# Right sides of the second token phase made ahead and kept in DRAM, and bias tables written by a job of their own

## The chip, the cores and the metric

The kernel runs on one core of a Trainium2 chip. TensorE (PE), VectorE (DVE), ScalarE (ACT), GpSimd (POOL) and SyncE (SP) each execute their instructions in the order of their own queue. The metric is device microseconds from one execution of the whole program.

## The reference

One step of a decoder layer for 1024 prompt tokens and 64 sample tokens of width 1024, 1088 columns in all. What matters here is the feed-forward block, which runs once before and once after the attention part:

```python
def _rmsnorm(x, g):
    y = xf * lax.rsqrt(jnp.mean(xf * xf, axis=-1, keepdims=True) + EPS)
    return (y * g.astype(jnp.float32)).astype(x.dtype)

def _swiglu(x, w_up, w_down):
    gate, up = jnp.split(x @ w_up, 2, axis=-1)
    return (jax.nn.silu(gate) * up) @ w_down
...
x = x + 0.5 * _swiglu(_rmsnorm(x, w["norm_ffn1"]), w["ffn1_w_up"], w["ffn1_w_down"])
... # attention with relative position bias, pooling, gates
x = x + 0.5 * _swiglu(_rmsnorm(x, w["norm_ffn2"]), w["ffn2_w_up"], w["ffn2_w_down"])
```

The attention adds a bias that is looked up in `rel_bias_table` by distance. Hidden width is 2816, everything is float32.

## The kernel before, in words

**Numbers.** A float32 operand is split into a rounded part and a rest (hi and lo, `split`, L217 on ACT and L218 on DVE or POOL), and a product is made of three matmuls, hi·hi, hi·lo and lo·hi (`mm3`, L271 to L273).

**Feed-forward block.** The residual `xt` lies transposed in SBUF, 8 blocks of 128 rows by 1088 columns. The columns are worked in two phases, `PHASES = ((0, 256), (512, 288))`: phase 0 takes columns 0 to 511 as two halves of 256, phase 1 columns 512 to 1087 as two halves of 288. Each phase runs over 22 units, 44 in the block; a unit takes 256 columns of the up weights, alternately of the gate and of the up half, and `jj` counts pairs of units, 0 to 21. A unit is a 2 × 2 block product in Strassen's manner, with 7 products instead of 8. Product q (0 to 6) multiplies a left side, a sum or difference of weight blocks, by a right side, a sum or difference of blocks of the normalised tokens; each is 12 matmuls (3 for each of k = 0 to 3), 84 a unit.

- *Left sides* are made by `prepare`, `LEAD = 5` products ahead of their use: at q = 0 POOL adds and subtracts (L435, L436), at q = 2 again (L439, L440), and each left side is rounded by ACT into `sh` and its rest made by DVE (`sl<-ur`, `sl<-s`, L218).
- *Right sides* are the same for all 22 units of a phase. `right_sides` makes them once at the start of a phase and keeps them in the SBUF buffers `h_hi` and `h_lo`, 7 q by 4 k by 256 or 288 columns. Per k it forms four halves (token block times gain times row scale, L382 on DVE, the row scale read from PSUM, where `over_rows`, L351, put it), four differences (L389, one on DVE and three on POOL) and seven splits (L394 on ACT, L395 on DVE, one of seven on POOL). So with phase 1 the whole of `h_hi`/`h_lo` is written anew, after the last product of phase 0 has read it. The sums of squares behind the phase-1 row scale (`sumsq`, L312 to L318) are made earlier, by two jobs started at `jj == 1`.
- *Results.* Products are combined on DVE (L516, L520, L522, L528, L529, L533) to the hidden values, which are split into `hh` and `hl` (`hl` on POOL). A pair of units later `down` multiplies them by the down weights into `psb`, in 512-column (phase 1: 288-column) matmuls, and L479 on DVE adds the sum to `xt`. After the last pair of phase 0 all its downs follow at once, and then `right_sides` of phase 1. SP issues the weight loads; `wh`/`wl` are down weights split by ACT and POOL.

`psa` and `psb` are PSUM tiles with four banks each, `tmp` a ring of eight SBUF tiles.

**Bias tables.** At the start `biases` makes four small matmuls (L570) of a one-hot table and `rel_bias_table`, copies them (`fr`, L572) and stores them to DRAM (`f_scr`, L573). From there POOL's queue issues 44 small DMAs into `b_scr` (L627, L629, L632, L635) and three larger ones into `f_rep` (L639), which the attention part reads long after the first block.

**What sets the order.** Python code emits instructions in program order, in which an `Interleaver` runs jobs beside the main code: its clock is advanced by the main code (0.36 us for a k of a product and so on), and a job that yields n is continued n us later on that clock. A scheduler then reorders the instructions of each engine by its own estimate of the time, so that the place in the code doesn't settle the place in a queue.

Of the kernel before, what the change touches and what calls it, by code (L numbers as in the profile page):

```python
# [11 lines left out]
F32 = mybir.dt.float32  # L12
F32R = mybir.dt.float32r
# [7 lines left out]
P = 128  # L21
# [98 lines left out]
def body(ctx, tc, x_prompt, x_sample, c128, c512, c2048, state_pool, rel_bias_table,  # L120
# [21 lines left out]
    def psa():  # L142
        return ps.tile([P, 512], F32, tag="a", name="psa")
# [39 lines left out]
    a_scr = dr.tile([P, 2, T], F32, name="a_scr")  # L183
    b_scr = dr.tile([3, NS, 4, 192], F32, name="b_scr")
    f_scr = dr.tile([4, 4, BL], F32, name="f_scr")
    f_rep = dr.tile([4, 4, P, BL], F32, name="f_rep")

    last_load = [None]
# [184 lines left out]
    def right_sides(xt, gi, p, rs):  # L373
# [23 lines left out]
        for k in range(4):  # L397
# [10 lines left out]
            parts(6, k, b22)  # L408
            parts(5, k, t4, G)

    def ffn(xt, gi, w_up, w_down, hook):


# [35 lines left out]
        def product(i, p):  # L449
            while made[0] <= i + LEAD:  # L450
                prepare(made[0])
                made[0] += 1
            lh, ll = left.pop(i)
            bank = psa()[:, :PHASES[p][1]]
            mm3(bank, [(lh[:, k, :], ll[:, k, :], *operand(p, i % 7, k)) for k in range(4)],
                0.36)
            il.advance(0.36)
            return bank
# [33 lines left out]

        load_unit(0)
        load_unit(1)
        prev = None
        for jj in range(22):
            p, j = divmod(jj, 11)
            t0, m = PHASES[p]
            if j == 0:
                if p:  # L500
                    right_sides(xt, gi, p, [over_rows(diagonal(st, m)) for st in sts])
                prev = None
            if jj == 1:
                sts = [stat() for _ in range(2)]
                for h in range(2):
                    il.spawn(sumsq(xt, PHASES[1][0] + h * PHASES[1][1], PHASES[1][1], sts[h]), 8 * h)
            hid = [fp.tile([P, 2, 576], F32R, tag=x, name=x, bufs=2) for x in ("hh", "hl")]
            sil = {}
            for kind in range(2):
# [30 lines left out]
                result(0, 1, product(7 * n + 6, p), b, False)  # L540
            prev = hid
            if j == 10 and p == 0:
                down_some(jj, prev, range(KD))
            elif j == 10:
                hook(jj, -1, 0)
                for i, (c0, n) in enumerate(chunks(1)):
                    for d in range(KD):
                        down(jj, prev, d, c0, n)
                        hook(jj, i, d)
# [30 lines left out]
    for t in range(ntile):  # L580
        rows = P if t < 8 else NS
        xn = ip.tile([P, D], F32, tag="xn", name="xn", bufs=7)
        load(xn[:rows], xp[t * P:(t + 1) * P, :] if t < 8 else xs)
        xns.append(xn)
    first = []
    for tiles in ((0, 1), (2, 3), (4, 5, 6, 7, 8)):
        for t in tiles:
# [27 lines left out]
        first.append(over_rows(dg))  # L615
        if tiles[0] == 2:
            right_sides(xt, 0, 0, first)
    biases()
    ictx.close()
    bctx.close()  # L620

    def fbias(g, off, ap):
        return bass.AP(tensor=f_scr.tensor, offset=f_scr.offset + g * 4 * BL + off, ap=ap)


    for g in range(3):
        G.dma_start(out=b_scr[g][:, :, P:], in_=neg.unsqueeze(1).to_broadcast([NS, 4, NS]))  # L627
        if g == 2:
            G.dma_start(out=b_scr[g][:, :, :P], in_=fbias(g, 127, [[0, NS], [BL, 4], [1, P]]))  # L629
        else:  # L630
            for q in range(Q):
                G.dma_start(out=b_scr[g][q::Q, :, :P],  # L632
                            in_=fbias(g, 127 - q // DIL[g], [[0, B], [BL, 4], [1, P]]))
        for b in range(B):
            G.dma_start(out=b_scr[g][b * Q:(b + 1) * Q, :, P + b * Q:P + (b + 1) * Q],  # L635
                        in_=fbias(g, 384, [[Q, Q], [BL, 4], [1, Q]]))

    for g in (0, 1, 3):
        G.dma_start(out=f_rep[g], in_=fbias(g, 0, [[BL, 4], [0, P], [1, BL]]))  # L639

    def spill(c):
        c0, n = CH[c]
# [794 lines left out]
```

## Time and profile before

| | |
|---|---|
| Median of 3 runs | 2520.71 us (2518.93 to 2524.88) |
| The profiled execution, own time | 2517.62 us |
| Its span, first to last instruction | 2515.9 us |
| Mean granted clock of TensorE | 0.953 |
| Busy: PE, DVE, POOL, ACT | 94%, 72%, 45%, 39% |
| First block, phase change | 438 to 494 us |
| Second block, phase change | 2068.4 to 2120.2 us |
| Up-weight loads | 176 of 512 KB, 3.9 us each to landing |
| Down-weight loads | 88 of 512 KB, 5.7 us each to landing |

Times are microseconds. The profiled execution stands beside the runs' median; durations are read from it. Busy shares are means over the whole span, and single stretches differ from them. The clock is given as a share of full speed (1 is 2.4 GHz, 0.5 is 1.2 GHz).

### The profile page before, as it was taken

What the parts mean: (1) busy time and instruction counts of PE and PEld (TensorE: products, weight loads), DVE (VectorE), ACT (ScalarE), POOL (GpSimd) and SP (SyncE); (2) the same over time, 40 slices, a digit from 0 to 9 for tenths busy, and PEclk for the clock granted to TensorE, in tenths of its full rate; (3) what the DMA queues carried; (4) which work ended last, traced back from release to release, by engine and by line L of the source; (5) the groups of instructions that cost most, each with busy time, mean ns of one, the idle gap of its engine ahead of it and who ended that gap; (6) DMA issues with size and microseconds to landing.
All of it is one profiled execution on the core that took longest, in us unless ns stands there. A gap on an engine that the chain in (4) does not pass through costs nothing. (4 is left out here: it accounts for less than half of the span.)

```text
span 2515.9 us, 42145 instructions
## 1 busy us (share of the span) xinstructions
PE 2363.3 (94%) x15894; PEld 2235.3 (89%) x15894; DVE 1817.6 (72%) x3246; ACT 975.9 (39%) x2130; POOL 1136.1 (45%) x1060
## 2 busy tenths in 40 slices
PE   4499999799999989999999999997999998999999
PEld 2489998699999989999999889996899987999998
DVE  5498888788888863366677424629988888788886
ACT  4244444343443433344333222214444443444442
POOL 6656666556555431201011110105666665566554
PEclk7799999799999989999899999997999997999999
DMA  6223343333324122457565773622244432333251
GB/s 189 78 80 109 109 134 134 124 101 118 118 101 134 50 68 83 152 163 233 181 193 177 244 233 118 217 76 75 88 140 140 152 138 68 126 127 127 92 201 38
DMA packets 208314, 328.72 MB, mean 131 GB/s; under 512 B 16272, under 2 KB 171600, under 8 KB 207328
## 3 DMA queue, kind: packets, MB, share of 16 engines
q1 hardware_dynamic: 194096, 293.48, 35.6%
q0 software_dynamic: 14016, 32.56, 3.7%
q8 instruction: 125, 2.05, 0.3%
q14 instruction: 77, 0.63, 0.1%
HBM read 297.10 MB, written 76.32 MB: 148 GB/s over the span
## 5 line engine op out<-in xcount | busy, mean ns | idle before, releaser
L271 PE MATMUL psa<-h_hi,sh 128*128 128x256 f32 (+1 forms) x2464 | 724.9, 295 | 62.1 <-ACT sh L217 51.0
L272 PE MATMUL psa<-h_lo,sh 128*128 128x256 f32 (+1 forms) x2464 | 727.9, 295 | 18.7 <-DVE h_lo L395 18.3
L273 PE MATMUL psa<-h_hi,sl 128*128 128x256 f32 (+1 forms) x2464 | 723.1, 294 | 0.0
L218 DVE TENSOR_TENSOR sl<-ur,sh 128x512 fp32r<-128x512 f32 x528 | 589.5, 1123 | 109.9 <-ACT sh L217 99.9
L271 PEld LDWEIGHTS psa<-h_hi,sh 128*128 128x128 f32 x2464 | 474.2, 193 | 77.4 <-ACT sh L217 52.8
L272 PEld LDWEIGHTS psa<-h_lo,sh 128*128 128x128 f32 x2464 | 474.7, 193 | 33.6 <-DVE h_lo L395 29.3
L273 PEld LDWEIGHTS psa<-h_hi,sl 128*128 128x128 f32 x2464 | 475.6, 193 | 0.5 <-DVE sl L218 0.5
L217 ACT ACTIVATE sh<-ur 128x512 fp32r<-128x512 f32 x528 | 330.3, 627 | 370.3 <-POOL ur L439 187.2
L272 PE MATMUL psa<-h_lo,wh 128*128 128x360 f32 (+1 forms) x1104 | 374.7, 339 | 5.5 <-DVE h_lo L364 5.5
L271 PE MATMUL psa<-h_hi,wh 128*128 128x360 f32 (+1 forms) x1104 | 376.6, 342 | 3.4 <-ACT h_hi L363 3.4
L273 PE MATMUL psa<-h_hi,wl 128*128 128x360 f32 (+1 forms) x1104 | 370.9, 336 | 0.0
L272 PE MATMUL psb<-hl,wh 128*128 128x288 f32 (+1 forms) x1056 | 349.0, 331 | 6.2 <-POOL hl L218 6.2
L271 PE MATMUL psb<-hh,wh 128*128 128x288 f32 (+1 forms) x1056 | 338.0, 336 | 13.3 <-ACT hh L217 11.5
L273 PE MATMUL psb<-hh,wl 128*128 128x288 f32 (+1 forms) x1056 | 348.5, 331 | 0.0
L218 POOL TENSOR_TENSOR hl<-tmp,hh 128x288 fp32r<-128x288 f32 (+1 forms) x176 | 171.7, 984 | 378.4 <-ACT hh L217 378.4
L479 DVE SCALAR_TENSOR_TENSOR xt<-psb,xt 128x288 f32<-128x288 f32 (+1 forms) x528 | 260.8, 526 | 76.2 <-PE psb L273 75.3
L218 POOL TENSOR_TENSOR wl<-wr,wh 128x512 fp32r<-128x512 f32 x176 | 259.0, 1492 | 93.5 <-ACT wh L217 49.2
L217 ACT ACTIVATE wh<-wr 128x512 fp32r<-128x512 f32 (+1 forms) x284 | 157.9, 615 | 177.9 <-PE psa L272 112.9
L272 PEld LDWEIGHTS psa<-h_lo,wh 128*128 128x128 f32 x1104 | 214.2, 194 | 10.3 <-DVE h_lo L364 5.8
L271 PEld LDWEIGHTS psa<-h_hi,wh 128*128 128x128 f32 x1104 | 213.6, 194 | 10.6 <-issue 5.0
L271 PEld LDWEIGHTS psb<-hh,wh 128*128 128x128 f32 x1056 | 194.9, 190 | 29.4 <-ACT hh L217 12.4
L272 PEld LDWEIGHTS psb<-hl,wh 128*128 128x128 f32 x1056 | 200.7, 190 | 22.4 <-POOL hl L218 8.6
(262 smaller groups left out, 3416.9 us busy)
## 6 DMA issues: line engine op xcount, KB each, us to landing
ur<-in_ffn_w_up_dram SPq DMA_DIRECT2D x176, 512.0 KB, 3.9
wr<-in_ffn_w_down_dram SPq DMA_DIRECT2D x88, 512.0 KB, 5.7
out_dram<-in_cache_kv_w_dram SPq DMA_DIRECT2D x32, 1020.0 KB, 7.6
qb<-q_scr SPq DMA_DIRECT2D x96, 256.0 KB, 4.4
wr<-in_w_in_dram SPq DMA_DIRECT2D x38, 512.0 KB, 4.7
kt<-in_cache_kv_w_dram SPq DMA_DIRECT2D x64, 256.0 KB, 4.3
vt<-in_cache_kv_w_dram SPq DMA_DIRECT2D x26, 512.0 KB, 7.9
t<-t_scr SPq DMA_DIRECT2D x16, 544.0 KB, 5.0
```

The lines of the kernel that those rows point to most:

```text
L217: S.activation(hi, src, AF.Copy)
L218: eng.tensor_tensor(out=lo, in0=src, in1=hi.bitcast(F32), op=ALU.subtract)
L271: PE.matmul(out, lh, rh, start=i == 0, stop=False)
L272: PE.matmul(out, lh, rl, start=False, stop=False)
L273: PE.matmul(out, ll, rh, start=False, stop=i == n - 1)
L479: V.scalar_tensor_tensor(out=xd, in0=o, scalar=0.5, in1=xd, op0=ALU.mult, op1=ALU.add)
```

## The change

**Right sides.** A new job `staged`, started at `jj == 1`, replaces the two `sumsq` jobs and the call of `right_sides` for phase 1. It makes the sums of squares, copies the row scale of each half from PSUM to an SBUF tile `rr`, and then forms per k, in three steps that yield 12 each, eight halves (L427: `b12` is formed three times, `b22` twice, `b11` twice, `b21` once), five differences (L433) and seven splits, all differences and rests on DVE. Each split goes to one of three rotating 288-column slots that lie in `h_hi`/`h_lo` behind the phase-0 right sides (28 × 256 = 7168 columns; the slots take 3 × 288 of the rest), and two DMAs on POOL's queue store it to a new DRAM tensor `r_scr` (144 KB each, 56 in a block). `recalled(q)` loads right side q into its place in `h_hi`/`h_lo`, two DMAs of 576 KB on POOL's queue: q = 0 to 4 before the products q = 2 to 6 of the last unit of phase 0, q = 5 and 6 after it. Both feed-forward blocks do so.

**Tables.** `biases` is called before the transposes of the tokens, and the 47 table DMAs are issued by a job `tables`, which starts 30 us into the interleaver's clock and yields 2 after each.

```diff
+    r_scr = dr.tile([2, 7, P, 4, PHASES[1][1]], F32R, name="r_scr")
...
+    def staged(xt, gi, rr):
+
+        t0, m = PHASES[1]
+        hi_, lo_ = [x.rearrange("p k t -> p (k t)") for x in (h_hi, h_lo)]
+        free = 28 * PHASES[0][1]
+        sts = [stat(), stat()]
+        for s in range(2):
+            yield from sumsq(xt, t0 + s * m, m, sts[s])
+            yield 8
+            V.tensor_copy(rr[:, s * m:(s + 1) * m], over_rows(diagonal(sts[s], m)))
+            yield 8
+        slot = [0]
+
+        def half(k, s):
+            h = tmp()[:, :m]
+            V.scalar_tensor_tensor(out=h, in0=xt[:, k, t0 + s * m:t0 + s * m + m],
+                                   scalar=gains[:, gi, k:k + 1], in1=rr[:, s * m:(s + 1) * m],
+                                   op0=ALU.mult, op1=ALU.mult)
+            return h
+
+        def less(a, b):
+            V.tensor_tensor(out=a, in0=a, in1=b, op=ALU.subtract)
+
+        def keep(q, k, h):
+            o = free + slot[0] % 3 * m
+            slot[0] += 1
+            hi, lo = hi_[:, o:o + m], lo_[:, o:o + m]
+            split(hi, lo, h)
+            G.dma_start(out=r_scr[0, q][:, k, :], in_=hi)
+            G.dma_start(out=r_scr[1, q][:, k, :], in_=lo)
+
+        for k in range(4):
+            b11, b12 = half(k, 0), half(k, 1)
+            keep(0, k, b11)
+            less(b12, b11)
+            keep(3, k, b12)
+            yield 12
+            b22, b12 = half(k + 4, 1), half(k, 1)
+            keep(6, k, b22)
+            less(b22, b12)
+            keep(4, k, b22)
+            yield 12
+            b22, b12 = half(k + 4, 1), half(k, 1)
+            less(b12, half(k, 0))
+            less(b22, b12)
+            keep(2, k, b22)
+            b21 = half(k + 4, 0)
+            keep(1, k, b21)
+            less(b21, b22)
+            keep(5, k, b21)
+            yield 12
+
+    def recalled(q):
+        m = PHASES[1][1]
+        for i, x in enumerate((h_hi, h_lo)):
+            G.dma_start(out=x.rearrange("p k t -> p (k t)")[:, 4 * q * m:4 * (q + 1) * m],
+                        in_=r_scr[i, q].rearrange("p k m -> p (k m)"))
...
             lh, ll = left.pop(i)
+            if 7 * 21 < i < 7 * 22:
+                recalled(i % 7 - 2) if i % 7 > 1 else None
...
             if j == 0:
-                if p:
-                    right_sides(xt, gi, p, [over_rows(diagonal(st, m)) for st in sts])
                 prev = None
             if jj == 1:
-                sts = [stat() for _ in range(2)]
-                for h in range(2):
-                    il.spawn(sumsq(xt, PHASES[1][0] + h * PHASES[1][1], PHASES[1][1], sts[h]), 8 * h)
+                job = il.spawn(staged(xt, gi, fp.tile([P, 576], F32, name="rr")))
+            if jj == 10:
+                il.finish(job)
...
             if j == 10 and p == 0:
+                recalled(5)
+                recalled(6)
                 down_some(jj, prev, range(KD))
...
+    biases()
     first = []
...
-    biases()
...
-    for g in (0, 1, 3):
-        G.dma_start(out=f_rep[g], in_=fbias(g, 0, [[BL, 4], [0, P], [1, BL]]))
+    def tables():
...
+        for g in (0, 1, 3):
+            G.dma_start(out=f_rep[g], in_=fbias(g, 0, [[BL, 4], [0, P], [1, BL]]))
+            yield 2
+
+    il.spawn(tables(), 30)
```

**Where the instructions come to stand.** The line numbers of the changed kernel are one higher up to the new functions and some 60 higher behind them: L218/L219 are its `split`, L272 to L274 its `mm3`, L390 and L396 the differences and rests of `right_sides`, L494, L495, L498, L499 the additions of the left sides, L540 the sum into `xt`, L575 to L592 the combinations, L690 to L705 the table writes.

At the start, on POOL, from the end of the table writes on; before (`s_497` and `ur` are weights and weight sums of the first unit):

```order
44 L635 DMA b_scr<-f_scr 32x1x8 x5
45 L629 DMA b_scr<-f_scr 256x1x128
46 L635 DMA b_scr<-f_scr 32x1x8 x7
47 L395 TENSOR_TENSOR h_lo<-tmp,h_hi 128x256
48 L635 DMA b_scr<-f_scr 32x1x8
49 L639 DMA f_rep<-f_scr 512x1x448 x2
50 L435 TENSOR_TENSOR s_497<-ur 128x512
51 L436 TENSOR_TENSOR ur<-ur 128x4x128
52 L439 TENSOR_TENSOR ur<-s_497,ur 128x4x128
53 L440 TENSOR_TENSOR ur<-ur 128x4x128
```

and in the changed kernel, where `s_451` is the sum of the first unit:

```order
33 L700 DMA b_scr<-f_scr 32x1x8 x5
34 L495 TENSOR_TENSOR ur<-ur 128x4x128
35 L700 DMA b_scr<-f_scr 32x1x8 x3
36 L396 TENSOR_TENSOR h_lo<-tmp,h_hi 128x256
37 L390 TENSOR_TENSOR tmp<-tmp 128x256
38 L705 DMA f_rep<-f_scr 512x1x448 x2
39 L390 TENSOR_TENSOR tmp<-tmp 128x256
40 L705 DMA f_rep<-f_scr 512x1x448
41 L498 TENSOR_TENSOR ur<-s_451,ur 128x4x128
42 L390 TENSOR_TENSOR tmp<-tmp 128x256 x2
43 L396 TENSOR_TENSOR h_lo<-tmp,h_hi 128x256
44 L499 TENSOR_TENSOR ur<-ur 128x4x128
```

The f_rep issues are still ahead of the second pair of additions of the first unit (L439 before, L498 now), and the differences and rests of the right sides, which stood among the table writes, now partly follow them.

In phase 0, on DVE, one unit from its last rest of a weight sum on; before:

```order
220 L218 TENSOR_TENSOR sl<-s_1723,sh 128x512
221 L479 SCALAR_TENSOR_TENSOR xt<-psb,xt 128x512 x4
222 L516 TENSOR_TENSOR si<-tmp,psa 128x256
223 L218 TENSOR_TENSOR sl<-ur,sh 128x512
224 L516 TENSOR_TENSOR si<-tmp,psa 128x256
225 L218 TENSOR_TENSOR sl<-ur,sh 128x512 x2
226 L520 TENSOR_TENSOR tmp<-tmp,psa 128x256
227 L522 TENSOR_TENSOR tmp<-tmp,si 128x256
228 L218 TENSOR_TENSOR sl<-ur,sh 128x512
229 L528 TENSOR_TENSOR tmp<-tmp,psa 128x256
230 L218 TENSOR_TENSOR sl<-ur,sh 128x512
```

and the same place of the changed kernel, a unit in which the job works:

```order
242 L219 TENSOR_TENSOR sl<-s_1745,sh 128x512
243 L219 TENSOR_TENSOR sl<-ur,sh 128x512
244 L540 SCALAR_TENSOR_TENSOR xt<-psb,xt 128x512
245 L219 TENSOR_TENSOR sl<-ur,sh 128x512
246 L540 SCALAR_TENSOR_TENSOR xt<-psb,xt 128x512 x3
247 L579 TENSOR_TENSOR tmp<-tmp,psa 128x256
248 L427 SCALAR_TENSOR_TENSOR tmp<-xt,gains,rr 128x288 x2
249 L581 TENSOR_TENSOR tmp<-tmp,si 128x256
250 L587 TENSOR_TENSOR tmp<-tmp,psa 128x256
251 L433 TENSOR_TENSOR tmp<-tmp 128x288
252 L219 TENSOR_TENSOR h_lo<-tmp,h_hi 128x288
253 L588 TENSOR_TENSOR tmp<-tmp,psa 128x256
```

Halves (L427), a difference (L433) and rests into the slots (`h_lo<-tmp,h_hi`) now stand between the combinations and the rests of the left sides. On POOL the two stores of each split stand between additions in the same way.

At the phase change of the first block, on PE, the last downs of phase 0 and what follows; before:

```order
2361 L271 MATMUL psb<-hh,wh 128x512
2362 L272 MATMUL psb<-hl,wh 128x512
2363 L273 MATMUL psb<-hh,wl 128x512
2364 L351 MATMUL psb<-tmp,ones 128x288 x2
2365 L271 MATMUL psa<-h_hi,sh 128x288 x2
2366 L272 MATMUL psa<-h_lo,sh 128x288
2367 L273 MATMUL psa<-h_hi,sl 128x288
2368 L272 MATMUL psa<-h_lo,sh 128x288
2369 L273 MATMUL psa<-h_hi,sl 128x288
```

and in the changed kernel:

```order
2341 L272 MATMUL psa<-h_hi,sh 128x288
2342 L273 MATMUL psa<-h_lo,sh 128x288
2343 L274 MATMUL psa<-h_hi,sl 128x288
2344 L272 MATMUL psb<-hh,wh 128x512 x4
2345 L272 MATMUL psa<-h_hi,sh 128x288
2346 L273 MATMUL psa<-h_lo,sh 128x288
2347 L274 MATMUL psa<-h_hi,sl 128x288
2348 L272 MATMUL psa<-h_hi,sh 128x288
2349 L273 MATMUL psa<-h_lo,sh 128x288
```

Product 0 of phase 1 (288 columns) now precedes downs of phase 0 (`psb`, 512 columns), which before came first, all 48 of them; five of the new phase's products stand ahead of the last of them. On POOL, at the same place, the loads into `h_hi` and `h_lo` in the changed kernel:

```order
238 L494 TENSOR_TENSOR s_4782<-ur 128x512
239 L495 TENSOR_TENSOR ur<-ur 128x4x128
240 L467 DMA h_lo<-r_scr 128x1152
241 L467 DMA h_hi<-r_scr 128x1152
242 L467 DMA h_lo<-r_scr 128x1152
243 L467 DMA h_hi<-r_scr 128x1152
244 L219 TENSOR_TENSOR hl<-tmp,hh 128x256
245 L498 TENSOR_TENSOR ur<-s_4782,ur 128x4x128
246 L467 DMA h_lo<-r_scr 128x1152
247 L467 DMA h_hi<-r_scr 128x1152
248 L499 TENSOR_TENSOR ur<-ur 128x4x128
249 L467 DMA h_lo<-r_scr 128x1152
```

They stand between the additions of the next units' left sides (L494 to L499) and the rests `hl` of the hidden values; the last four come some nine rows later, behind four `wl`. Before, differences and rests of the right sides stood there.

## Rows read from the trace of the kernel before

**Rows 1.** Page: busy time of each engine; PE's busy tenths in 40 slices.
```profile
PE 2363.3 (94%) x15894; PEld 2235.3 (89%) x15894; DVE 1817.6 (72%) x3246; ACT 975.9 (39%) x2130; POOL 1136.1 (45%) x1060
...
PE   4499999799999989999999999997999998999999
```

**Rows 2.** Timeline of PE near 96 us: start, us, instruction, [idle before <-releaser].
```profile
95.80 0.58 PE L271 MATMUL psa<-h_hi,sh 128*128 128x256 f32 x1 [35.39 <-ACT sh L217]
```

**Rows 3.** Timeline of POOL, 18 to 95 us.
```profile
18.89 2.69 POOL L218 TENSOR_TENSOR wl<-wr,wh 128x512 fp32r<-128x512 f32 x2 [8.07 <-ACT wh L217]
...
36.56 3.35 POOL L632 DMA_DIRECT2D b_scr<-f_scr  x6 [0.72 <-DMA f_scr<-fr]
...
50.11 0.76 POOL L389 TENSOR_TENSOR tmp<-tmp 128x256 f32<-128x256 f32 x1
...
64.58 0.55 POOL L632 DMA_DIRECT2D b_scr<-f_scr  x1 [9.96 <-DMA f_rep<-f_scr]
...
90.03 1.09 POOL L639 DMA_DIRECT2D f_rep<-f_scr  x1 [11.59 <-issue]
91.13 1.28 POOL L435 TENSOR_TENSOR s<-ur 128x512 f32<-128x512 f32 x1
```

**Rows 4.** Windows: us, PE PEld DVE ACT POOL busy (x), clock, DMA share, GB/s.
```profile
438.00:494.00 56.00, 38.87 (x142) 29.69 (x142) 44.60 (x68) 19.74 (x45) 31.09 (x31) 0.73 0.34 120
200.00:420.00 220.00, 220.00 (x1523) 204.38 (x1522) 186.50 (x284) 99.72 (x197) 148.03 (x112) 1.00 0.37 123
520.00:840.00 320.00, 320.00 (x2392) 318.13 (x2391) 269.38 (x435) 130.64 (x252) 184.49 (x144) 1.00 0.33 112
```

**Rows 5.** Windows of PE's psa instructions (two rows), then of its psb instructions (one).
```profile
438.00:494.00 56.00, 23.86 (x90) 0.73 0.34 120
2068.40:2120.20 51.80, 21.79 (x68) 0.67 0.29 102
...
438.00:494.00 56.00, 15.01 (x52) 0.73 0.34 120
```

**Rows 6.** Timeline of PE around the first phase change.
```profile
442.63 1.66 PE L271 MATMUL psb<-hh,wh 128*128 128x512 f32 x4 [4.58 <-ACT hh L217]
445.91 0.79 PE L272 MATMUL psb<-hl,wh 128*128 128x512 f32 x1 [1.62 <-POOL hl L218]
...
450.42 0.40 PE L273 MATMUL psb<-hh,wl 128*128 128x512 f32 x1
...
457.90 0.40 PE L273 MATMUL psb<-hh,wl 128*128 128x512 f32 x1
458.13 1.13 PE L351 MATMUL psb<-tmp,ones 128*128 128x288 f32 x4
```

**Rows 7.** Timeline of DVE at the same place.
```profile
458.94 1.78 DVE L382 SCALAR_TENSOR_TENSOR tmp<-xt,gains,psb 128x288 f32<-128x288 f32 x4
...
468.38 0.45 DVE L395 TENSOR_TENSOR h_lo<-tmp,h_hi 128x288 fp32r<-128x288 f32 x1
```

**Rows 8.** DVE's groups, 438 to 494: count | busy us, mean ns | idle before.
```profile
L395 DVE TENSOR_TENSOR h_lo<-tmp,h_hi 128x288 fp32r<-128x288 f32 x24 | 19.7, 859 | 0.0
```

**Rows 9.** Groups of DVE's instructions, 200 to 420.
```profile
L218 DVE TENSOR_TENSOR sl<-ur,sh 128x512 fp32r<-128x512 f32 x85 | 93.9, 1111 | 11.8 <-ACT sh L217 11.0
...
L522 DVE TENSOR_TENSOR tmp<-tmp,si 128x256 f32<-128x256 f32 x28 | 16.7, 596 | 0.7
L520 DVE TENSOR_TENSOR tmp<-tmp,psa 128x256 f32<-128x256 f32 x28 | 11.7, 418 | 10.4 <-PE psa L273 10.4
```

**Rows 10.** Line L218, 200 to 420: duration ns min/median/max.
```profile
L218 DVE TENSOR_TENSOR sl<-ur,sh x85: 678/900/1810, 199.3 to 417.2; 128x512 fp32r<-128x512 f32 x85
...
L218 POOL TENSOR_TENSOR hl<-tmp,hh x28: 736/963/1201, 209.0 to 413.6; 128x256 fp32r<-128x256 f32 x28
L218 POOL TENSOR_TENSOR wl<-wr,wh x28: 1291/1610/1744, 218.1 to 410.7; 128x512 fp32r<-128x512 f32 x28
```

**Rows 11.** Windows, the first 20 us (columns as in rows 4).
```profile
0.00:20.00 20.00, 9.18 (x45) 7.98 (x46) 9.27 (x45) 10.08 (x18) 8.81 (x17) 1.00 0.93 297
```

More of the change, by code (lines that the diff above doesn't have):

```diff
@@ L494, in ffn @@
         load_unit(1)
-        prev = None
+        prev = job = None
         for jj in range(22):
@@ L623, in fbias @@
         return bass.AP(tensor=f_scr.tensor, offset=f_scr.offset + g * 4 * BL + off, ap=ap)
[L626 to L636, printed above, removed]
-    for g in (0, 1, 3):
-        G.dma_start(out=f_rep[g], in_=fbias(g, 0, [[BL, 4], [0, P], [1, BL]]))
+    def tables():
+        for g in range(3):
+            G.dma_start(out=b_scr[g][:, :, P:], in_=neg.unsqueeze(1).to_broadcast([NS, 4, NS]))
+            if g == 2:
+                G.dma_start(out=b_scr[g][:, :, :P], in_=fbias(g, 127, [[0, NS], [BL, 4], [1, P]]))
+                yield 2
+            else:
+                for q in range(Q):
+                    G.dma_start(out=b_scr[g][q::Q, :, :P],
+                                in_=fbias(g, 127 - q // DIL[g], [[0, B], [BL, 4], [1, P]]))
+                    yield 2
+            for b in range(B):
+                G.dma_start(out=b_scr[g][b * Q:(b + 1) * Q, :, P + b * Q:P + (b + 1) * Q],
+                            in_=fbias(g, 384, [[Q, Q], [BL, 4], [1, Q]]))
+                yield 2
+        for g in (0, 1, 3):
+            G.dma_start(out=f_rep[g], in_=fbias(g, 0, [[BL, 4], [0, P], [1, BL]]))
+            yield 2
+    il.spawn(tables(), 30)
     def spill(c):
```

## The prediction

> **What bounds the kernel now.** I read the page first: TensorE (PE) is busy 94% of the span, VectorE (DVE) 72%, GpSimd (POOL) 45% [rows 1]. A PE that is nearly always busy is shortened only where it stands still or runs at the lower clock, and the slices say where: the first two, one in each feed-forward block at its change of token phase, and the two ends of the middle part [rows 1]. The change touches three such places.
>
> *The start.* PE's timeline shows a wait of 35.39 us up to 95.80, for a left side that ScalarE (ACT) rounds [rows 2]. The timeline of POOL shows why. Left sides of products 2 onward need the additions L435 to L439, and these stand on POOL behind the table writes: b_scr issues of 0.55 us each, the first f_rep issue, then 9.96 us of waiting for its transfer, more issues, a second wait of 11.59 us ahead of the last f_rep issue, and only at 91.13 the first L435 [rows 3].
>
> *The two phase changes.* In the window 438–494 PE works 38.87 us of 56.00 at a mean granted clock of 0.73; in its twin, 2068.4–2120.2, the clock is 0.67 [rows 4, 5]. The reader should first ask what this work costs at full speed. From 520 to 840 PE is busy without a gap, with 2392 matmuls of 288 columns: 320/2392 = 0.134 us each [rows 4]. The 33 down matmuls of 512 columns from 450.42 to 457.90 stand 7.48/32 = 0.234 us apart [rows 6]. The first window holds 90 product matmuls and 52 on psb, four of them L351 and 48 downs, so 90 × 0.134 + 48 × 0.234 = 23.3 us; the second has 68 and, by the code, again 48 downs, so 9.1 + 11.2 = 20.3 [rows 5, 6]. Lost are **32.7 and 31.5 us**. The timeline puts it in three pieces: 4.58 and 1.62 us for the hidden values; downs at the lower clock until about 450; and after the downs (458.13) the products wait for right sides that DVE only begins to make at 458.94 [rows 6, 7]. DVE is the chain there: its 24 roundings L395 take 859 ns in the mean, where one alone takes 0.45 us [rows 7, 8].
>
> *Phase 0 itself*, where the change puts the work. From 200 to 420 PE never stops (220.00 of 220.00), but DVE is busy 186.50 us, and POOL 148.03 [rows 4]. L522 runs twice a unit, and 28 of them make 14 units of 15.7 us [rows 9]. So DVE is idle 33.5/14 = 2.4 us a unit. Part of its busy time is waiting: the rounding sl<-ur takes 678 ns at best, 1111 in the mean, 1810 at most, while L520, the same kind of instruction with one operand in PSUM, stays at 418; L522, with both operands in SBUF, takes 596 [rows 9, 10]. I read this as DVE's instructions with two SBUF operands being held up while POOL runs one.
>
> **The change part by part.**
>
> *Tables.* The job is meant to spread the 44 + 3 issues; the order says otherwise. All still stand at the start of POOL's queue, now in front of L498 of unit 0, and much of the right sides' work of k = 2 and 3 is pushed behind them. Sum: six wl roundings of about 1.35 us from 18.89 end near 27; 45 small issues × 0.55 = 24.8; three f_rep × 1.1 = 3.3; two waits as before, 9.96 + 11.59; seven roundings and additions of 256 columns × 0.75 and two additions of 512 × 1.28, together 7.8; 2.6 left for the wait on the inputs of the first additions, an estimate; L498 itself 1.3: it ends near 88, where L439, two behind the L435 of 91.13, ended near 95 [rows 3]. Some ten right-side and left-side instructions are still to come behind it, 9 to 11 us, so full work begins near 98, against 95.80 [rows 2, 3]. I take **+2 us**; bounds −12 (the second wait falls away) and +10 (both waits grow by a third, about 7, and the first products start later). The four bias matmuls are earlier and cost nothing while PE waits for inputs.
>
> *Work added to phase 0, in each block.* Per k 8 halves L427, 5 subtractions L433, 7 roundings: 80 instructions on DVE, at 0.445 us for a half (four in 1.78) and 0.45 or less for the others [rows 7]: with the ends overlapping the next start, 32 × 0.445 + 48 × 0.37 = 32 us. In before, the halves read the row scale from PSUM; now rr lies in SBUF, so every one of the 80 has two SBUF operands. What each waits for POOL no row shows; the nearest are L522, 596 − 418 = 178 ns, and sl<-ur, 1111 − 678 = 433 ns [rows 9, 10]. I take 260, nearer L522, which is as short: 21 us. In the order nine preparation quads, about 9.7 units or 152 us, lie between the first and the last store, and DVE's idle time there is 9.7 × 2.4 = 23. PE has left sides for five products and four banks in hand; I count three products, 3 × 15.7/7 = 6.6 us, as absorbed once. What is then too much stretches the phase, and a stretched phase meets less of POOL per us, which I take as 15% of all held-up time (21 for the new ones and 9.7 × 3.0 for those there, six sl and two L522 a unit), 8 us. So 32 + 21 − 23 − 6.6 − 8 = **15 us** a block; bounds 0 (no hold-up at all: 32 − 23 − 6.6 = 2.5, with a little more in hand) and 33 (433 ns each, nothing in hand). The 28 ACT roundings cost nothing: ACT is busy under half [rows 1]. The 56 stores cost POOL 56 × 0.55 = 31 us over 152 [rows 3], and POOL has a third idle [rows 4]; but each waits in POOL's queue for its rounding, with the next additions behind it.
>
> *Taken from the phase change.* Gone are 16 halves, 4 subtractions and 24 roundings on DVE, 28 roundings on ACT, 16 instructions on POOL, two L351 pairs. In their place 14 loads, 7 × 2 × 128 × 1152 × 4 bytes = 8.26 MB. The fullest stretch, 0–20, moved 297 GB/s [rows 11]: 28 us; with what is loaded there already, 20 us at the 120 GB/s of 438–494 [rows 4], 2.4 MB, 36 us. The order puts the first loads behind L495 of unit 22, near 430, hence the last land near 466. PE wants the last right side near 438 + 11.2 (downs) + 11.3 (seven products) = 460. PE's order now has five products before the last downs, so a late load blocks those downs too. Left over: 6 us late and some 3 of lower clock, 9 of about 32. I take **−23 us** at each change; bounds −15 (the old hidden-value wait, 6.2, and a clock as low as now for half of the work, 11) and −29.
>
> *Sum:* +2 + 2 × 15 − 2 × 23 = −14 against this execution's own 2517.6 us; the runs' median is 3.1 higher, so **2507 us**.
>
> **A rule weighed against the trace.** POOL takes most of DVE's free time in phase 0: by rows, two wl of 1.291, two hl of 0.736 and four additions of 1.28 make 9.2 of a unit's 15.7 us, 58% [rows 3, 10]; sl's 678 to 1810 ns fits a wait for one whole POOL instruction. The Trainium skill, page "SBUF — State Buffer", section "Who interferes with whom", calls the shared port pair an exclusive lock: a DVE instruction with two SBUF inputs and a GpSimd one that reads SBUF block each other fully, and one with a single SBUF input does not. It speaks against the copy of rr to SBUF; the trace agrees as far as sl, L522 and L520 go. If each of the 80 meets a POOL instruction with chance 0.58 and waits half of one of some 1.2 us, it loses 0.35 us rather than 0.26: 28 us instead of 21, a loss of 22 a block (32 + 28 − 23 − 6.6 − 8.5), and a total of 2507 + 2 × 7 = 2521, no gain at all. Rival 1 takes this in.
>
> **The rivals.**
> 1. *DVE saturates in phase 0* (slower). Held up like sl<-ur, 433 ns each, the 80 cost 32 + 35 − 23 − 6.6 − 10 = 27 us a block [rows 9, 10]: 2507 + 24 = 2531; with 0.35 us each, 2521. It decides once a block loses more than (46 − 2)/2 = 22. For it: DVE already at 85%; against: hold-ups shrink when the phase stretches.
> 2. *The loads come late.* They stand on POOL's queue between additions and roundings, and behind PE's reads of the same buffer. If the change loses 20 us instead of 9: 2507 + 22 = 2529. Against it: POOL has little else to do there, its busy time is 31.09 us of 56, some of it the removed part [rows 4].
> 3. *Phase 0 absorbs the work:* 2.5 a block instead of 15, 2482. For it: DVE has 23 us free and left sides run five products ahead.
> 4. *The tables do leave the start* (the change does what its words say, against the order): the 35.4 us wait goes, 2507 − 35 = 2472 [rows 2].
>
> **How the numbers follow.** Measurement tells about 0.2% (5 us) from no change. Forecast (2495 to 2518) 0.38, of which 0.30 faster and 0.08 same; rival 1 0.22, slower; rival 2 0.14, same 0.06 and slower 0.08; rival 3 0.16 and rival 4 0.10, faster. Faster 0.56, same 0.14, slower 0.30. The range runs from rival 4 to a little beyond rival 1: 2470 to 2540; the forecast's own is 2495 to 2518.
>
> **What would show it.** Right: sl<-ur and L522 longer than before over some 150 us of phase 0, PE waiting there a few times for left sides; at the changes PE at 0.9 or more of the window and no wait for h_lo on DVE; all f_rep issues still before the first L498. Wrong: PE full through the staging (rival 3); PE waiting for r_scr loads by more than 10 us (rival 2); no 35 us wait in the first 100 us (rival 4). What would upset the sum most is POOL's in-order queue: a store that waits for its rounding while DVE waits for POOL, a convoy, whose price no row here gives.

## The result and the profile after

The changed kernel takes **2547.38 us** (2546.11 to 2549.28), against 2520.71: a ratio of 1.0103, 95% interval 1.0081 to 1.0126. It is 27 us slower, where 14 faster was forecast, and above the range. Its profiled execution spans 2547.3 us at a clock of 0.957.

PE does the same work; the page shows DVE busy for 74 us more than in [rows 1], and where PE's slices lost:

```profile
PE 2367.8 (93%) x15894; PEld 2242.3 (88%) x15894; DVE 1891.7 (74%) x3322; ACT 968.6 (38%) x2130; POOL 1174.4 (46%) x1168
...
PE   4488889999999989999999999997988899999999
```

The slice of the first phase change, the eighth, rises from 7 to 9; the third to the sixth fell from 9 to 8, and three slices of the second block as well. To turn this into microseconds, one instruction was followed through both traces: DVE's first L516 (L575 in the changed kernel) of each pair of units, and how much later it starts than in the kernel before. The differences between places are what each stage costs.

| place in the program | before, us | changed, later by | of this stage | forecast |
|---|---|---|---|---|
| block 1, pair 1 (start) | 128.0 | 4.5 | +4.5 | +2 |
| block 1, pair 10 (end of phase 0) | 412.9 | 48.6 | **+44.1** | +15 |
| block 1, pair 13 (phase 1) | 547.6 | 19.5 | **−29.1** | −23 |
| block 2, its first pair | 1732.5 | 17.3 | −2.2 | 0 |
| block 2, pair 10 | 2043.5 | 58.3 | **+41.0** | +15 |
| block 2, pair 13 | 2177.7 | 31.8 | **−26.5** | −23 |

So the phase changes gave more than forecast, and phase 0 took almost three times as much.

*The start.* POOL's timeline of the changed kernel, to be held against [rows 3]:

```profile
64.12 1.14 POOL L705 DMA_DIRECT2D f_rep<-f_scr  x1
76.60 1.11 POOL L705 DMA_DIRECT2D f_rep<-f_scr  x1 [11.34 <-issue]
...
89.14 1.09 POOL L705 DMA_DIRECT2D f_rep<-f_scr  x1 [10.68 <-issue]
90.25 1.27 POOL L498 TENSOR_TENSOR ur<-s,ur 128x512 f32<-128x512 f32 x1
```

The three f_rep issues stand as the order had them, and POOL stands still between them, 11.34 and 10.68 us; L498 ends at 91.5.

*The phase change.* The window that begins 48.6 us after 438 and holds the same downs (48) and nearly as many products (84) as in [rows 4, 5]:

```profile
486.60:513.60 27.00, 23.95 (x132) 21.36 (x131) 18.65 (x23) 7.80 (x17) 17.61 (x18) 0.94 0.80 277
```

At full speed 84 × 0.134 + 48 × 0.234 = 22.5 us; 4.5 of 27 are lost, against 32.7 of 56, and PE's only listed wait there is for a load:

```profile
PE psa L272 <- DMA h_hi<-r_scr: 3.1, 1, 3.1
```

*Phase 0.* Between the same two places (pairs 2 and 8) the kernel before needs 188 us and the changed one 230:

```profile
163.00:351.00 188.00, 186.60 (x1295) 173.34 (x1294) 158.04 (x242) 85.43 (x168) 128.29 (x98) 1.00 0.36 120
```

```profile
169.00:399.00 230.00, 198.58 (x1287) 180.32 (x1288) 218.66 (x330) 91.31 (x196) 151.36 (x151) 0.96 0.43 129
```

DVE's busy time rises from 158.04 to 218.66, its idle time falls from 30 to 11.3: 60.6 more work and hold-up, 18.6 of it into idle time, 42 into the length. For PE the same 42 us are 30.0 more of standing still (31.4 against 1.4) and 12.0 more of work, at a mean granted clock of 0.96 instead of 1.00. DVE's groups, as in [rows 9] (mean ns of one):

```profile
L219 DVE TENSOR_TENSOR sl<-ur,sh 128x512 fp32r<-128x512 f32 x73 | 81.5, 1131 | 6.0 <-ACT sh L218 5.7
...
L427 DVE SCALAR_TENSOR_TENSOR tmp<-xt,gains,rr 128x288 f32<-128x288 f32 x32 | 22.2, 731 | 0.0
L219 DVE TENSOR_TENSOR h_lo<-tmp,h_hi 128x288 fp32r<-128x288 f32 x28 | 22.0, 787 | 0.0
L581 DVE TENSOR_TENSOR tmp<-tmp,si 128x256 f32<-128x256 f32 x24 | 18.8, 787 | 0.2
L433 DVE TENSOR_TENSOR tmp<-tmp 128x288 f32<-128x288 f32 x20 | 14.6, 732 | 0.0
```

The three groups of the job (L427, the rests h_lo, L433) take 58.8 us. In this sum overlaps are counted twice, since each instruction starts some 0.07 us before the one ahead has ended; timed from that end, as the 53 of the prediction were, the 80 take **54** us. L581, which was L522, takes 787 ns instead of 596. One stretch of the two timelines shows what a hold-up is, first DVE:

```profile
195.43 4.27 DVE L219 TENSOR_TENSOR h_lo<-tmp,h_hi 128x288 fp32r<-128x288 f32 x1
199.63 0.68 DVE L540 SCALAR_TENSOR_TENSOR xt<-psb,xt 128x512 f32<-128x512 f32 x1
200.23 3.17 DVE L433 TENSOR_TENSOR tmp<-tmp 128x288 f32<-128x288 f32 x1
```

and POOL at the same time:

```profile
194.90 1.31 POOL L219 TENSOR_TENSOR wl<-wr,wh 128x512 fp32r<-128x512 f32 x1
196.16 1.29 POOL L494 TENSOR_TENSOR s<-ur 128x512 f32<-128x512 f32 x1
197.41 1.28 POOL L219 TENSOR_TENSOR wl<-wr,wh 128x512 fp32r<-128x512 f32 x1
198.66 0.73 POOL L219 TENSOR_TENSOR hl<-tmp,hh 128x256 fp32r<-128x256 f32 x1
```

A rest that takes 0.45 us alone [rows 7] starts at 195.43 and ends at 199.70, 0.31 us after POOL's string of four instructions without a gap (199.39). It was not let in between two of them.

### The profile page after: what moved, and what is told of

It is laid out like the page before. It is cut to its first block, busy times and chain, and to the rows that moved or that the text cites. A ratio compares the mean times of both kernels' runs of the same rounds, so it can differ in the third digit from the quotient of the medians.

```text
span 2547.3 us, 42461 instructions
## 1 busy us (share of the span) xinstructions
PE 2367.8 (93%) x15894; PEld 2242.3 (88%) x15894; DVE 1891.7 (74%) x3322; ACT 968.6 (38%) x2130; POOL 1174.4 (46%) x1168
## 5 line engine op out<-in xcount | busy, mean ns | idle before, releaser
L272 PE MATMUL psa<-h_hi,sh 128*128 128x256 f32 (+1 forms) x2464 | 729.6, 297 | 85.6 <-ACT sh L218 33.6
L274 PE MATMUL psa<-h_hi,sl 128*128 128x256 f32 (+1 forms) x2464 | 725.6, 295 | 9.0 <-DVE sl L219 9.0
L219 DVE TENSOR_TENSOR sl<-ur,sh 128x512 fp32r<-128x512 f32 x528 | 586.3, 1118 | 100.1 <-ACT sh L218 86.4
L272 PEld LDWEIGHTS psa<-h_hi,sh 128*128 128x128 f32 x2464 | 477.9, 194 | 101.7 <-ACT sh L218 38.9
L273 PEld LDWEIGHTS psa<-h_lo,sh 128*128 128x128 f32 x2464 | 478.6, 194 | 16.3 <-DVE h_lo L396 12.4
L274 PEld LDWEIGHTS psa<-h_hi,sl 128*128 128x128 f32 x2464 | 477.6, 194 | 12.0 <-DVE sl L219 11.5
L218 ACT ACTIVATE sh<-ur 128x512 fp32r<-128x512 f32 x528 | 325.3, 624 | 299.9 <-POOL ur L498 146.5
L272 PE MATMUL psa<-h_hi,wh 128*128 128x360 f32 (+1 forms) x1104 | 374.7, 340 | 3.1 <-ACT h_hi L364 3.1
L274 PE MATMUL psa<-h_hi,wl 128*128 128x360 f32 (+1 forms) x1104 | 369.5, 335 | 0.0
L272 PE MATMUL psb<-hh,wh 128*128 128x288 f32 (+1 forms) x1056 | 340.1, 338 | 16.0 <-ACT hh L218 14.4
L274 PE MATMUL psb<-hh,wl 128*128 128x288 f32 (+1 forms) x1056 | 347.7, 330 | 0.0
L219 POOL TENSOR_TENSOR hl<-tmp,hh 128x288 fp32r<-128x288 f32 (+1 forms) x176 | 167.3, 958 | 298.8 <-ACT hh L218 298.2
L540 DVE SCALAR_TENSOR_TENSOR xt<-psb,xt 128x288 f32<-128x288 f32 (+1 forms) x528 | 261.3, 525 | 55.5 <-PE psb L274 54.6
L219 POOL TENSOR_TENSOR wl<-wr,wh 128x512 fp32r<-128x512 f32 x176 | 255.4, 1474 | 67.5 <-DVE xt L1418 42.0
L272 PEld LDWEIGHTS psb<-hh,wh 128*128 128x128 f32 x1056 | 196.0, 191 | 34.4 <-ACT hh L218 16.0
L218 ACT ACTIVATE wh<-wr 128x512 fp32r<-128x512 f32 (+1 forms) x284 | 157.8, 615 | 177.6 <-PE psa L273 114.6
L494 POOL TENSOR_TENSOR s<-ur 128x512 f32<-128x512 f32 x88 | 120.6, 1371 | 221.1 <-DVE sl L219 108.3
L272 PEld LDWEIGHTS psa<-h_hi,wh 128*128 128x128 f32 x1104 | 212.4, 193 | 10.3 <-issue 4.9
```

What stands on the lines that cost most here:

```text
L218: S.activation(hi, src, AF.Copy)
L219: eng.tensor_tensor(out=lo, in0=src, in1=hi.bitcast(F32), op=ALU.subtract)
L272: PE.matmul(out, lh, rh, start=i == 0, stop=False)
L273: PE.matmul(out, lh, rl, start=False, stop=False)
L274: PE.matmul(out, ll, rh, start=False, stop=i == n - 1)
L494: G.tensor_tensor(out=s1s[n], in0=a21, in1=a22, op=ALU.add)
```

## The experiments

Two theories of the loss in phase 0 stood against each other: **A**, VectorE has no time left there, by the job's own instructions and by their hold-ups; **B**, the stores and their waits in GpSimd's in-order queue hold up the additions and the hidden values' rests behind them. Three more of the start: **D** and **F**, the table writes, or the standstill of the queue at the f_rep issues, hold the first left sides back; **E**, the right sides of phase 0 do so anyway.

All twelve runs, with the ratio to the kernel before measured beside it (its 95% interval), and how much later than in the kernel before the same places come. b1 and b2 are the blocks; the cost of a stage is the difference of two columns.

| run | median, us | ratio | b1 pair 1 | b1 pair 10 | b1 pair 13 | b2 first | b2 pair 10 | b2 pair 13 |
|---|---|---|---|---|---|---|---|---|
| e1 staged only | 2552.96 | 1.0136 (1.0114–1.0158) | 0.9 | 46.4 | 17.1 | 19.5 | 61.4 | 33.3 |
| e2 tables only | 2512.13 | 0.9978 (0.9968–0.9989) | 6.7 | 6.7 | 6.9 | −0.8 | −0.9 | −1.8 |
| e3 stores on SP | 2525.50 | 1.0030 (1.0012–1.0048) | 4.3 | 36.5 | 7.1 | −0.2 | 34.8 | 8.2 |
| e4 spread | 2554.72 | 1.0142 (1.0126–1.0157) | 4.9 | 45.8 | 19.9 | 20.2 | 64.3 | 38.1 |
| e5 60 instead of 80, stores on SP | 2507.28 | 0.9957 (0.9937–0.9977) | 5.1 | 26.1 | 0.3 | −10.2 | 12.9 | −15.3 |
| e6 tables tied behind additions | 2515.49 | 0.9993 (0.9984–1.0003) | −31.3 | 2.1 | 1.1 | −1.5 | −0.1 | −0.2 |
| e7 e5 and e6 | 2504.86 | 0.9952 (0.9939–0.9966) | −32.4 | 17.4 | −4.0 | −11.2 | 12.2 | −8.6 |
| e8 halves read PSUM | 2540.72 (one run) | – | 4.2 | 42.0 | 14.4 | 13.9 | 50.6 | 23.1 |
| e9 tables on SP | 2489.13 | 0.9886 (0.9869–0.9902) | −34.0 | −19.6 | −20.1 | −29.8 | −29.7 | −29.7 |
| e10 e5 and e9 | 2482.04 | 0.9864 (0.9843–0.9886) | −33.0 | 7.7 | −21.5 | −30.7 | −6.3 | −36.1 |
| e11 e9, f_rep apart | 2475.16 | 0.9825 (0.9812–0.9839) | −33.0 | −34.1 | −35.3 | −44.7 | −44.7 | −44.9 |
| e12 e10, f_rep apart | 2465.35 | 0.9801 (0.9779–0.9823) | −33.4 | −12.4 | −42.1 | −46.1 | −20.9 | −40.0 |

**e1, e2: the two parts of the change.** e1 is the changed kernel with `biases` and the table writes where they were; e2 is the kernel before with these two moved.

> The staged right sides alone; the tables are written as in the kernel before. Theory A (the parts add up): the first units stood 4.5 us later in the changed kernel than in the kernel before, so this one is 4 to 5 us faster than the changed kernel, 2543 us, and its phase 0 is stretched by the same 41 to 44 us in each block. Rival (the moved table writes or the matmuls moved ahead disturb more than the start): over 10 us faster than the changed kernel, below 2537.

> The tables' job and the earlier bias matmuls alone, on the kernel before. Theory A: 4 to 5 us slower than before, 2525 us, because the issues still stand ahead of the first left sides and push right-side work behind them. Rival (the job does spread them when nothing else is changed): the 35 us wait at the start is gone and the time is near 2490.

The whole loss is the staging's: phase 0 is stretched by 45.5 and 41.9 us without the tables too. The tables alone cost some 6 us at the start, yet the whole is 0.2% faster: between the two blocks 7.7 us come back (7.3 in e3), but only 2.2 in the changed kernel, and in e1 2.4 more are lost. The changes shift the order in the attention part a little as well; what in it gains stays open. Both expectations missed, e1 by 10 and e2 by 13 us; the stretch between the blocks, which neither had counted, is 4.6 us of the one (against the changed kernel) and 7.7 of the other.

**e3: stores on SP.** The edit:

```diff
-            G.dma_start(out=r_scr[0, q][:, k, :], in_=hi)
-            G.dma_start(out=r_scr[1, q][:, k, :], in_=lo)
+            nc.sync.dma_start(out=r_scr[0, q][:, k, :].bitcast(F32), in_=hi.bitcast(F32))
+            nc.sync.dma_start(out=r_scr[1, q][:, k, :].bitcast(F32), in_=lo.bitcast(F32))
```

> The changed kernel, with the 56 stores of each block issued by SP instead of POOL. Theory A (VectorE has no time left in phase 0: 80 instructions with two SBUF operands, held up behind whole strings of GpSimd work, some 65 us with what they add to others, against 23 us of idle time): phase 0 is still stretched by 35 to 45 us in each block, 2530 to 2548 us. Theory B (GpSimd's queue: 31 us of issues and the waits of each store for its rounding hold up the additions and hidden-value rests behind them): the stretch falls to 20 us or less in each block, about 2500 us.

The stretch falls from 44 and 41 to 32 and 35 us: between the two theories, nearer to the first. Its phase 0 between pairs 2 and 8, and its rest sl:

```profile
169.10:387.50 218.40, 194.39 (x1289) 175.91 (x1290) 207.21 (x330) 92.70 (x196) 125.42 (x95) 0.98 0.42 138
```

```profile
L219 DVE TENSOR_TENSOR sl<-ur,sh 128x512 fp32r<-128x512 f32 x73 | 73.5, 1009 | 6.1 <-ACT sh L218 5.7
...
L427 DVE SCALAR_TENSOR_TENSOR tmp<-xt,gains,rr 128x288 f32<-128x288 f32 x32 | 26.2, 865 | 0.0
```

DVE is busy 11.5 us less than in the changed kernel, with about the same idle time (11.2 us); 8 of these are sl's, down to 1009 ns in the mean. The halves gain nothing (865). What went are the longest hold-ups. All sl of this stretch (min/median/max, ns), in the changed kernel and in e3:

```profile
L219 DVE TENSOR_TENSOR sl<-ur,sh x73: 674/692/5239, 168.6 to 397.7; 128x512 fp32r<-128x512 f32 x73
```

```profile
L219 DVE TENSOR_TENSOR sl<-ur,sh x73: 678/693/1783, 168.5 to 385.8; 128x512 fp32r<-128x512 f32 x73
```

In the changed kernel eight DVE instructions of the stretch take over 2 us; in e3, and in e5 below, none takes over 1.79. So the waits of several us come with the stores in POOL's queue, and what is right in theory B acts through DVE's time.

**e4: the same work over more units.** `yield 12` becomes `yield 20` in the three steps.

> The changed kernel, with 20 instead of 12 yielded between the steps of the job, so that the same work lies over some 16 units instead of 9.7. Theory A (VectorE's time): the same demand of 65 us meets 16 x 2.4 = 38 us of idle time instead of 23, so each block loses about 15 us less, 2517 us. Theory B (each store and each hand-over costs its own delay in an in-order queue): the loss goes with the number of steps and stays, 2545 us or more.

No gain: 40.9 and 44.1 us, the outcome forecast for theory B. Pairs 2 to 10, 249.7 us in the kernel before with DVE busy 210.69, become (the groups below from 169 to 440):

```profile
169.70:458.70 289.00, 262.24 (x1724) 239.43 (x1725) 274.21 (x410) 119.57 (x252) 196.58 (x184) 0.96 0.44 133
```

```profile
L427 DVE SCALAR_TENSOR_TENSOR tmp<-xt,gains,rr 128x288 f32<-128x288 f32 x30 | 29.7, 1032 | 0.0
L581 DVE TENSOR_TENSOR tmp<-tmp,si 128x256 f32<-128x256 f32 x29 | 26.9, 928 | 0.3
```

Idle time falls from 39.0 to 14.8, so 24 us of room were used instead of 18.6. But the demand rose with it, from 60.6 to 63.5: halves now take 1032 ns, L581 928. And the room left does not lie where the work is. First a step of the job and what follows it, then the next step's end up to the step after:

```profile
296.20:319.00 22.80, 18.81 (x126) 17.60 (x125) 22.80 (x33) 8.89 (x19) 17.14 (x17) 0.93 0.39 113
322.10:346.20 24.10, 24.10 (x164) 22.08 (x162) 21.53 (x32) 11.01 (x23) 17.43 (x15) 1.00 0.27 76
```

From 296.2 DVE has no idle time at all (22.80 of 22.80) and PE stands still for 4 us; later DVE is idle for 2.6 us and PE loses nothing. 367.1 to 390.0 and 394.9 to 418.0 show the same (DVE 22.90 of 22.90 and 21.76 of 23.10). The expectation had counted all idle time as usable and the demand as fixed; both were wrong: `yield 20` moved the steps apart and left each as dense as it was. Its time alone would also fit theory B; that DVE is full where PE loses speaks for A. A job whose instructions are spread one by one was not run.

**e5: fewer instructions.** On e3, each half made once, `b22` in an SBUF tile of its own, 4 subtractions: 60 instructions a block.

```diff
         for k in range(4):
             b11, b12 = half(k, 0), half(k, 1)
+            half(k + 4, 1, bs)
+            t3 = tmp()[:, :m]
+            V.tensor_tensor(out=t3, in0=bs, in1=b12, op=ALU.subtract)
             keep(0, k, b11)
             less(b12, b11)
             keep(3, k, b12)
-            yield 12
...
+            keep(4, k, t3)
+            keep(6, k, bs)
+            less(bs, b12)
+            yield 18
+            keep(2, k, bs)
             b21 = half(k + 4, 0)
             keep(1, k, b21)
-            less(b21, b22)
+            less(b21, bs)
             keep(5, k, b21)
-            yield 12
+            yield 18
```

> As with the stores on SP, and the job's 80 VectorE instructions a block cut to 60 (each half made once, one SBUF tile kept for b22, 4 subtractions instead of 5 per k). Theory A (phase 0 stretches by what the job takes of VectorE, own time and hold-ups): with the stores on SP the 80 stretched it by some 33 us a block, so 60 stretch it by 33 x 60/80 = 25 or less, and the whole is 2525 - 2 x 8 = 2509 us, about 9 us faster than before. Rival C (PE loses at the bursts, whatever their size): the stretch stays within 4 us of 33, 2525 us.

Right: 21 and 23 us of stretch, and 0.43% faster than the kernel before. The edit also makes 8 steps of 12, so e5 alone cannot tell a loss by instruction from a loss by step. e3 and e8 (below) keep the 12 steps. Between pairs 2 and 8 the changed kernel takes 230.0 us with DVE busy 218.7, e3 218.4 with 207.2, e5 207.6 with 196.3, e8 223.9 with 212.4: 11.2 to 11.5 us apart in all four. The loss goes with DVE's busy time. Of the 15 us by which e5's profiled execution is ahead of the kernel before, about 5 come in each block and 10.5 between the blocks, where the cause is open.

**e8: what the second SBUF operand costs.**

```diff
         for k in range(4):
+            scales()
             b11, b12 = half(k, 0), half(k, 1)
...
-                                   scalar=gains[:, gi, k:k + 1], in1=rr[:, s * m:(s + 1) * m],
+                                   scalar=gains[:, gi, k:k + 1], in1=rs[s],
```

> The changed kernel, with the row scale read from PSUM: rr keeps the diagonal, and each step of the job spreads it over the rows anew (24 more L352 matmuls a block, some 7 us of PE). The 32 halves then have one SBUF operand. Theory A (hold-up comes with the second SBUF operand): their mean falls from 731 ns to 510 or less with no long one, and the rests and subtractions, which keep two, stay above 620. Rival (a half is held up by something else): it stays near 730. The time itself says little: 7 us less on VectorE, 7 more on PE, within 10 us of the changed kernel.

```profile
L433 DVE SCALAR_TENSOR_TENSOR tmp<-xt,gains,psb x32: 500/503/513, 179.5 to 349.3; 128x288 f32<-128x288 f32 x32
```

```profile
L439 DVE TENSOR_TENSOR tmp<-tmp x20: 445/452/7428, 180.4 to 357.8; 128x288 f32<-128x288 f32 x20
```

Halves (L433 here) with the row scale in PSUM take 500 to 513 ns, all 32 of them; the subtractions (L439), with both operands in SBUF, take up to 7428, and 1031 in the mean. The halves of the changed kernel, the same instruction with the same sizes, took up to 1990 ns, 731 in the mean:

```profile
L427 DVE SCALAR_TENSOR_TENSOR tmp<-xt,gains,rr x32: 503/507/1990, 174.4 to 355.4; 128x288 f32<-128x288 f32 x32
```

In spite of 7 us more of PE a block (24 L352 at 0.28, as the four L351 in [rows 6]), the blocks are stretched by 37.8 and 36.7 instead of 44.1 and 41.0 us.

**e6, e7, e9 to e12: the tables.** e6 ties each table DMA behind POOL's last addition so far; e9 gives them to SP, behind its last weight load; e11 puts 40 between the f_rep copies (the edit as it stands in e12, against the changed kernel).

```diff
+    def late_dma(out, in_):
+        with tc.issue_after(last_load[0].ins):
+            nc.sync.dma_start(out=out, in_=in_)
...
-            G.dma_start(out=f_rep[g], in_=fbias(g, 0, [[BL, 4], [0, P], [1, BL]]))
-            yield 2
+            late_dma(out=f_rep[g], in_=fbias(g, 0, [[BL, 4], [0, P], [1, BL]]))
+            yield 40
```

(e6 has `issue_after` the addition at q = 2 and `G.dma_start`, e9 `yield 2`.)

> The kernel before with the tables' job alone, each table DMA tied behind the last addition of the left sides on GpSimd, so that the order can't draw it to the start. Theory D (the table writes hold the first left sides back): the wait of 35 us at the start shrinks to under 12 us, and the whole is 20 to 35 us faster than the kernel before, 2483 to 2498. Rival E (the right sides of the first phase on VectorE and GpSimd are the chain there, the tables only stand in front): under 8 us faster.

> The two edits before together: 60 instructions, stores on SP, tables tied behind the additions. If the parts add up: 9 us from the first and 20 to 35 us from the second, 2474 to 2489 us, faster than both kernels. If the tables' issues, now in GpSimd's queue during the staging, hold up additions as the stores did, some 10 us of it is lost again.

> The kernel before with the tables' job, its 47 DMAs issued by SP behind the latest weight load. Theory F (the start was only late because GpSimd's queue stood still for some 22 us at the three f_rep issues; tied behind the additions the same 24 us came back at 218 to 243 us, and off that queue they are gone): the first units stay 31 us earlier, there is no wait above 10 us of PE in phase 0, and the whole is 25 to 33 us faster than the kernel before, 2484 to 2492 us. Rival (SP holds the weight loads back behind the table DMAs, or the transfers themselves cost): under 12 us faster.

> The changed kernel with 60 instead of 80 VectorE instructions, the stores on SP and the tables' DMAs on SP, spread. If the parts add up, the 10 us of the first two (against the kernel before) and the 25 to 33 of the third: 2474 to 2484 us. If SP's queue, in which a store waits for its rounding, now delays weight loads: 2495 or more.

> The kernel before with the tables on SP, and 40 instead of 2 yielded between the three f_rep copies, so that weight loads stand between them. If the loss of 14 us near 230 us came from weight loads that waited behind three copies in a row, it shrinks to 5 us or less: 10 us faster than with the copies together, 2479 us. If each copy delays loads on its own, the same 14 us are lost in three pieces: 2489 us.

> The best version so far (60 instructions, stores and tables on SP) with the same 40 between the f_rep copies. If that loss and the staging add up, 8 to 12 us faster than without, 2470 to 2474 us; if the staging has filled the place anyway, the same 2482 us.

e6 has 31 us in hand after the start and has lost them by pair 6. POOL there:

```profile
216.38 1.11 POOL L629 DMA_DIRECT2D f_rep<-f_scr  x1
229.82 1.10 POOL L629 DMA_DIRECT2D f_rep<-f_scr  x1 [12.33 <-issue]
242.29 1.08 POOL L629 DMA_DIRECT2D f_rep<-f_scr  x1 [11.37 <-issue]
```

The 24 us that POOL stands still at the three f_rep issues have only moved into a place where PE needs POOL; the expectation counted on the start alone, and the time is that of rival E for another reason. With the issues on SP (e9) POOL has none to stand still at, and the whole is 1.14% faster. But now SP's own queue stands still, 22 us over the three issues and the load behind them, where a load's issue takes some 0.35 us elsewhere:

```profile
195.15 11.73 SPq L628 DMA_DIRECT2D f_rep<-f_scr  x3
206.98 10.38 SPq L191 DMA_DIRECT2D wr<-in_ffn_w_down_dram  x1
```

14 of the 34 us of the start are lost near 228 us, where ACT waits for weights that were queued behind the three copies:

```profile
227.90 0.63 ACT L217 ACTIVATE sh<-ur 128x512 fp32r<-128x512 f32 x1 [8.29 <-DMA ur<-in_ffn_w_up_dram]
```

With loads between the copies (e11) an f_rep issue takes 0.6 us and the load behind it at most 2.8, and the loss is gone: 1.75% faster than the kernel before. On top of that the staging with 60 instructions gives 1.99% (e12), but the two intervals overlap, so the staging's own share is not settled: in the profiled execution of e12, the slowest of its five, its two phases cost 21.0 and 25.2 us and its two changes give 29.7 and 19.1. e9 and e10 came out within the times expected, e11 and e12 4 and 5 us below them; e7 did not (16 us too slow, 6 beyond its own reserve of 10), since its tables stall POOL's queue as in e6.

## Why the prediction was wrong

*The step that failed is "Work added to phase 0, in each block"*, sized at 15 us with an upper bound of 33; it measured 44 and 41. Its price of the work itself was right: own time and hold-up of the 80 instructions were reckoned at 32 + 21 = 53 us and took 54 between pairs 2 and 8 of the changed kernel. What failed are the three deductions, 37.6 us in all, of which 12 came:

- *Other instructions held up less*, −8: measured +6.6 (60.6 − 54). L581 rose from 596 to 787 ns, sl did not fall, and some 3 us are instructions for the job's second row scale, which fall into this window and lay ahead of it in the kernel before.
- *Idle time used*, 23: measured 18.6.
- *Left sides in hand*, 6.6: there is no room for them, 54 + 6.6 − 18.6 = 42 is the whole stretch.

Relief and slack make 21 of the 26.6 us of error. Relief assumed that POOL's instructions thin out; e4 shows the opposite, longer hold-ups at a lower density of the job.

*Rival 1, DVE saturates, was the right mechanism* with too small a price, 27; its deciding point, 22 us a block, was passed. Its hold-up of 35 us was more than the 22 measured (54 − 32), and its deductions of 39.6 were too large by more. e3, e5 and e8 each take a part of DVE's demand away and shorten the phase; e4, which takes none, does not.

*The rule weighed against the trace* pointed the right way. The Trainium skill, page "SBUF — State Buffer", section "Who interferes with whom", says that a DVE instruction with two SBUF inputs and GpSimd's reads exclude each other for whole instructions, and that one with a single SBUF input, outside the two-port modes, is free: e8 agrees, 503 ns with never a long one. Half of one POOL instruction each, 28 us, was somewhat more than the 22 measured; the 22 a block that came of it was too low by the same deductions. The mean hides the shape: half of the 32 halves took 507 ns or less, and the rest h_lo at 195.43 waited for four POOL instructions.

*Stores and loads.* "The 56 stores cost POOL 31 us, and POOL has a third idle" was too light: off POOL's queue they give back 12 and 6 us of stretch, and the longest hold-ups with them (e3). The prediction's last sentence named this, a convoy whose price no row gave. Rival 2 did not happen: the loads came 3.1 us late, not 20.

*The phase change* (−23) was right in mechanism and gave 29 and 26.5. *The tables* (+2): the order was read rightly, +4.5 measured; e1 and e2 put the part between 3.6 and 6.7. Rival 4's 35 us exist (e9, e11: 33 to 34); with the issues later on POOL's queue they are lost again (e6).

*The sum:* 4.5 + 44.1 − 29.1 − 2.2 + 41.0 − 26.5 = 31.8 us against a span longer by 31.4; the medians differ by 26.7.

## What to carry to other kernels

Work moved into a stage in which the bound engine never waits is not free if a second engine there is at 85%. Price that engine's own time and hold-ups, and take off idle time only where it lies beside the work: here the price was right to 1 us and the deductions were too large by 25.6. A busy share over a long stretch does not say whether an engine is full; look at the steps. A VectorE operand left in PSUM instead of copied to SBUF was out of GpSimd's way. A transfer that stalls its queue is not cured by issuing it later on the same queue, and on another queue it stalls that one; what cured it was another queue with loads between the large copies. Whether spacing alone would have done on GpSimd's queue was not run.

## What the runs showed of the hardware that was not expected

- A held-up VectorE instruction can wait for a string of GpSimd instructions, not one: 4.27 us over four of them in the changed kernel, up to 7.43 us in e8, over five and two store issues. With the stores on SP (e3, e5) none between pairs 2 and 8 took over 1.79 us.
- VectorE's busy share between pairs 2 and 10 of e4 is 95%, but 100% from 296.2 to 319.0, where PE loses time, and 89% from 322.1 to 346.2, where PE loses none.
- After an f_rep issue (896 KB) GpSimd's queue stands still for 10.7 to 12.3 us before the next, in the changed kernel and in e6; the stores (144 KB) and the loads of r_scr (576 KB) take some 0.55 us each to issue and don't stall it.
- Three copies of 896 KB in a row held SP's queue for 22 us, with the load behind them taking 10.38 us to issue, and ACT waited 8.29 us for weights.
